# Which attention heads of a hybrid decoder layer get turned exponentials

## The chip, the cores and the metric

One core of one Trainium2 chip runs the whole layer. The metric is the device time of one execution in microseconds (us); lower is better. The profiled execution has a span (first to last instruction) and a time of its own, which is a little longer.

## The reference, cut to what matters

One decoder layer on `x` of 2048 tokens by 1024 channels. After an RMS norm one input projection feeds three head groups, each with a SiLU gate; their gated outputs are mapped back by an output projection and added to `x`.

```python
# eight causal heads of 64 channels, with a forget gate
logits = (q . k) / sqrt(64) + F[t] - F[s]        # F = cumsum(log sigmoid(f)), only s <= t
y_b = softmax(logits) @ v
# four memory heads: every query reads 256 memory tokens
y_m = softmax((q_m . k_m) / sqrt(64)) @ v_m
# a pooling mixer, four groups
y = x + concat(y_a * silu(g_a), y_b * silu(g_b), y_m * silu(g_m)) @ w_out
```

All of it is float32; the kernel keeps that precision by splitting operands into a high and a low fp16 half.

## The kernel before, in words

The work is cut into 16 units n = (p, j): four passes p, each with two causal heads (h = 0 and h = 1) and one memory head (h = 2), and in each pass four query blocks j of 512 queries. `proj` computes one unit's projections on TensorE (`mm3`, L721: tiles `pa` of 512 columns and `pb` of 256). `attention` then takes the three heads of a unit in the order 2, 0, 1. After the last unit comes the output projection (`po`, also L721), whose early part is placed beside the last attention units.

A causal head in block j has 16j + 10 score blocks of 128 queries by 128 keys that lie on or below the diagonal: 10, 26, 42 and 58. A memory head has 8. A head is softened in one of two ways.

**The normal way** (`scores`, `soften`). Queries lie on the partitions, keys in the free dimension. TensorE writes a PSUM tile `q` of up to 1024 score columns with two matmuls per piece of up to 512 columns (L1250 and L1256: the high half and the correction), and the diagonal blocks get a mask matmul (L1253). VectorE takes the minimum of each row (L1273), `nm` is made from it (L1281, L1277), and ScalarE takes the exponential with `nm` as its bias (L1288). `halves` splits the result into a high half (L1308 on VectorE or L1311 on ScalarE) and a low half (L1315 on VectorE or GpSimd), both in a tile `ph`. The weighting with the values needs keys on the partitions, so a DMA transposes `ph` to `pt` (L1324), issued from SyncE's queue, and only then do the `pv` matmuls of `weigh` (L1353 to L1355, three for each block) run. Heads of j >= 2 are softened in two groups of keys (the first 1024, and the rest), which are joined at the end with a factor `al` (L1296, L1298, L1371, L1386).

**The turned way** (`scores` with `peak=True`, `peak`, `turned_scores`, `spread`). The scores are written twice. First with queries on the partitions and the high half alone (L1250 and the mask, no L1256), only to take the row minima (L1180, L1184); when all pieces of the head have been read, the minima of two groups are merged (L1194), scaled into two rows `mz` (L1196, L1197), transposed by four matmuls into `mp` (L1204) and copied into two spare rows of the query tile (L1208). Then the scores are written again with keys on the partitions (`columns`, L1166 and L1170, the mask at L1168), so that the minimum is subtracted by the matmul itself and the exponential (L1223) needs no bias of its own per query. The split halves in `ph` are already in the form that `weigh` wants: no transpose by DMA, no `pt`, and one group of keys.

`turned(j, h)` chooses the way. It is read where the heads are listed (L1431), and by `follow` (L1516), which sets how fast attention is paced against the projections.

The order of all work is planned at build time by `Order`, a simulation with a cost for each engine and for SyncE's queue (`COST`, L40); instructions are then issued in the planned order, and each engine runs its own list in order. TensorE's list merges `lead` (projections) and `follow` (attention) with a lag of 1.1 units. `AHEAD = 1` lets the minima pass of the next head be issued while the current head is still in its exponentials:

```python
            for ahead in todo[:self.AHEAD + 1]:
                ...
                if ahead["todo"]:
                    step = ahead
                    break
```

Score tiles `q` have two buffers, `ph` nine, `pt` six, and up to `DEEP = 7` parts wait in the queue `late` before their `pv` matmuls are drained, first in, first out. SyncE's queue also issues the loads of `x`, of the weights, the stores and the transposes of `Q`, `K` and the mixed rows. When the three heads of a unit are finished, `store_mixed` casts and stores the unit's mixed rows (L1531, two casts per unit).

Of the kernel before, what the change touches and what calls it, by code (L numbers as in the profile page):

```python
# [201 lines left out]
class Layer:  # L202
# [932 lines left out]

    def turned(self, j, h):

        return h == 2 or j < 2

    def columns(self, j, h):  # L1140

# [269 lines left out]
    def attention(self):  # L1411
# [15 lines left out]
        def heads():  # L1427
            for n in range(n_units):
                p, j = divmod(n, NJ)
                for h in (2, 0, 1):  # L1430
                    turned = self.turned(j, h)  # L1431
                    peaks = self.pieces(j, h)
                    pieces = self.columns(j, h) if turned else peaks
                    subs, count = [], 0
                    for piece in pieces:
                        subs.append([])
                        for sub in piece if turned else self.cut(piece):
                            subs[-1].append((count, sub))
                            count += 1
                    yield {  # L1440
                        "n": n, "h": h, "turned": turned, "todo": list(enumerate(peaks)) if turned else [], "peaks": len(peaks),
                        "rest": list(enumerate(pieces)), "pv": {}, "box": {}, "subs": subs, "count": count, "last": h == 1,
                        "flat": [sub for group in subs for _, sub in group],
                    }
# [310 lines left out]
```

## Time and profile before

| what | value |
|---|---|
| time, median of 3 runs | 1100.43 us (1099.67 to 1102.37) |
| the profiled execution: time | 1099.49 us |
| the profiled execution: span | 1097.6 us |
| TensorE busy | 1019.0 us, 93% |
| VectorE busy | 821.7 us, 75% |
| ScalarE busy | 563.6 us, 51% |
| GpSimd busy | 454.7 us, 41% |
| the DMA queue of SyncE | 76.2% of the 16 engines' span |
| mean granted TensorE clock | 0.990 |

Busy shares are means over stages with different limits, and the end of a matmul in the trace is modelled, so a stretch in which TensorE is busy need not be one at its full rate. The work of one pass alternates between light attention (blocks 0 and 1) and heavy attention (blocks 2 and 3), so the views are read by such stretches.

### The profile page before, as it was taken

The numbers are of one execution on the slowest core, as the hardware profiler recorded it, in microseconds if no ns is written. First come the engines' busy times: TensorE is split into PE (matmuls) and PEld (weight loads), VectorE is DVE, ScalarE is ACT, GpSimd is POOL, SyncE is SP. The second block draws the span as 40 slices with busy tenths as digits, with TensorE's granted clock in tenths as the row PEclk, the third lists the DMA queues.
The fourth block names the chain that finished last, engine by engine and source line by source line (L and its number), as shares of the span: only waits on it lengthen the run. The fifth ranks groups of instructions, "written<-read, shape, count | busy, mean of one in ns | idle before, by whom it ended". The sixth has DMA issues, their size and how long they took to land.

```text
span 1097.6 us, 23751 instructions
## 1 busy us (share of the span) xinstructions
PE 1019.0 (93%) x8981; PEld 615.1 (56%) x8981; DVE 821.7 (75%) x1894; ACT 563.6 (51%) x1424; POOL 454.7 (41%) x504
## 2 busy tenths in 40 slices
PE   6799998899889998898999999989999979999998
PEld 2355655556556565565565655556656645554443
DVE  6976879996987986969987969799796895761111
ACT  4775757665555455647544656655555663430000
POOL 6654636444544544535443434444533351221000
PEclk9999999999999999999999999999999999999999
DMA  9988677895996627969968159899692696998521
GB/s 280 222 213 190 181 220 189 211 185 124 199 205 172 172 79 131 180 144 180 198 182 217 40 113 182 192 212 199 196 222 62 143 209 168 226 219 215 182 96 48
DMA packets 375361, 192.05 MB, mean 175 GB/s; under 512 B 331792, under 2 KB 339920, under 8 KB 374224
## 3 DMA queue, kind: packets, MB, share of 16 engines
q1 hardware_dynamic: 375104, 190.54, 76.2%
q8 instruction: 70, 1.15, 0.4%
q14 instruction: 43, 0.35, 0.1%
q10 hardware_dynamic: 144, 0.01, 0.0%
HBM read 84.23 MB, written 25.26 MB: 100 GB/s over the span
## 4 chain that ended last, share of the span: by engine, by line
PE 34%; DVE 20%; DMA 11%; issue 4%; POOL 2%; ACT 2%; SPq 1%; DVEq 0%; ACTq 0%; POOLq 0%
PE po L721 13%; DMA pt<-ph 9%; PE pa L721 7%; PE pb L721 6%; DVE mn L1273 4%; DVE ph L1315 4%; DVE ph L1308 2%; PE q L1250 2%; PE pv L1353 2%; PE pv L1355 1%; DMA w1a<-in_w_a 1%; PE pv L1354 1%; DVE mn L1184 1%; PE q L1256 1%; DVE qq L1013 1%
## 5 line engine op out<-in xcount | busy, mean ns | idle before, releaser
L721 PEld LDWEIGHTS <-x 128*128 128x128 f16 x2304 | 216.3, 98 | 131.2 <-issue 3.8
L721 PE MATMUL pa<-ah,x 128*128 128x512 f16 x768 | 250.0, 381 | 0.4 <-DVE z L960 0.4
L1315 POOL TENSOR_TENSOR ph<-p,ph 128x512 f16<-128x512 f32 (+3 forms) x114 | 134.7, 1185 | 240.0 <-DVE ph L1308 117.6
L1288 ACT ACTIVATE p<-q,nm 128x512 f32<-128x512 f32 (+1 forms) x224 | 135.4, 644 | 124.7 <-DVE nm L1277 52.5
L721 PE MATMUL po<-aho,om 128*128 128x512 f16 x512 | 159.2, 381 | 2.9 <-DVE xo L1619 2.9
L1315 DVE TENSOR_TENSOR ph<-p,ph 128x512 f16<-128x512 f32 (+2 forms) x214 | 149.1, 716 | 2.4 <-ACT ph L1311 1.4
L721 PE MATMUL pa<-al,x 128*128 128x512 f16 x384 | 146.2, 381 | 0.0
L1273 DVE TENSOR_REDUCE mn<-q 128x1 f32<-128x1024 f32 (+7 forms) x128 | 124.6, 983 | 27.9 <-PE q L1256 27.7
L721 PE MATMUL pb<-bh,x 128*128 128x256 f16 x768 | 142.0, 273 | 1.3 <-DVE v L940 1.3
L1353 PE MATMUL pv<-v,pt 128*128 128x65 f16 x800 | 94.6, 194 | 33.2 <-DMA pt<-ph 32.5
L721 PEld LDWEIGHTS <-om 128*128 128x128 f16 x768 | 73.5, 98 | 87.1 <-issue 4.1
L1353 PEld LDWEIGHTS <-pt 128*128 128x128 f16 x800 | 74.9, 98 | 60.3 <-DMA pt<-ph 49.4
L1250 PE MATMUL q<-k,q 67*128 67x512 f16 (+2 forms) x320 | 104.6, 350 | 3.4 <-DVE mn L1184 1.4
L721 PE MATMUL pb<-bl,x 128*128 128x256 f16 x384 | 104.9, 273 | 0.0
L985 POOL TENSOR_TENSOR rr<-ss,mhalf 128x10 f32<-128x10 f32 x32 | 63.7, 1990 | 98.2 <-DVE ss L980 83.2
L721 PE MATMUL po<-alo,om 128*128 128x512 f16 x256 | 97.5, 381 | 0.0
L1405 POOL TENSOR_TENSOR gate<-gate,hy 128x128 f32<-128x128 f32 x96 | 51.7, 558 | 106.4 <-DVE hy L1396 96.3
L1354 PE MATMUL pv<-v,pt 128*128 128x64 f16 x800 | 94.1, 194 | 0.0
L1355 PE MATMUL pv<-v,pt 128*128 128x65 f16 x800 | 93.8, 194 | 0.0
L1619 DVE SCALAR_TENSOR_TENSOR xo<-po,So_p,xo 128x512 f32<-128x512 f32 x32 | 23.9, 748 | 92.1 <-PE po L721 92.1
L721 PEld LDWEIGHTS <-xx 128*128 128x128 f16 x720 | 68.0, 98 | 42.9 <-PE pa L745 1.2
L1311 ACT CAST ph<-p 128x512 f16<-128x512 f32 (+2 forms) x162 | 90.6, 584 | 1.6
(275 smaller groups left out, 2292.8 us busy)
## 6 DMA issues: line engine op xcount, KB each, us to landing
x<-xd SPq DMA_DIRECT2D x48, 512.0 KB, 5.7
xrx<-in_x SPq DMA_DIRECT2D x16, 512.0 KB
xd<-xx SPq DMA_DIRECT2D x16, 512.0 KB, 6.3
md<-mt SPq DMA_DIRECT2D x32, 256.0 KB, 2.3
om<-md SPq DMA_DIRECT2D x8, 1024.0 KB
xo<-in_x SPq DMA_DIRECT2D x16, 512.0 KB, 6.2
out_dram<-xo SPq DMA_DIRECT2D x32, 256.0 KB, 3.4
w0a<-in_w_a SPq DMA_DIRECT2D x12, 512.0 KB, 4.9
```

Of the source, the lines that this page charges most:

```text
L721: nc.tensor.matmul(out, rows, r[kt][:, :ncol], start=(kt == 0 and i == 0), stop=(kt == KT - 1 and i == 2))
L985: nc.gpsimd.tensor_tensor(rr, ss, self.mhalf[:, 0:10].rearrange("p (a b) -> p a b", b=5), op=ALU.pow)
L1250: nc.tensor.matmul(out, q1, kb, start=bank not in used, stop=peak and not diag, **kw)
L1273: nc.vector.tensor_reduce(mn[:, g, i:i + 1], qk[:, off:off + w], axis=AX.X, op=ALU.min)
L1288: nc.scalar.activation(p32[:, at:at + w], qk[:, off:off + w], AF.Exp, bias=nm[:, g, i:i + 1], scale=-1.0)
L1311: nc.scalar.copy(hl[:, :w], p32[:, :w])
L1315: (nc.vector if eng == "V" else nc.gpsimd).tensor_tensor(hl[:, w:2 * w], p32[:, :w], hl[:, :w], op=ALU.subtract)
L1353: nc.tensor.matmul(pv[:, i, :], ph, hi, start=start and b == 0, stop=False, **kw)
L1354: nc.tensor.matmul(pv[:, i, 0:HD], ph, v[:, 0:HD], start=False, stop=False, **kw)
L1355: nc.tensor.matmul(pv[:, i, :], pl, hi, start=False, stop=end and b == nb - 1, **kw)
L1405: nc.gpsimd.tensor_tensor(gate, gate, y[:, 2 * u:2 * u + 2, 0:HD], op=ALU.mult)
L1619: nc.vector.scalar_tensor_tensor(xr[:, t, :], pj, self.So, xr[:, t, :], op0=ALU.mult, op1=ALU.add)
```

## The change

One line. The memory heads stay turned. Before, both causal heads of blocks 0 and 1 were turned and both of blocks 2 and 3 normal. After it, the first causal head (h = 0) of blocks 1, 2 and 3 is turned, and the second head of every block and both heads of block 0 are normal.

```diff
     def turned(self, j, h):
 
-        return h == 2 or j < 2
+        return h == 2 or (h == 0 and j > 0)
```

## Rows read from the trace of the kernel before

**Rows 1.** The page: the span and the busy time of each engine.
```profile
span 1097.6 us, 23751 instructions
PE 1019.0 (93%) x8981; PEld 615.1 (56%) x8981; DVE 821.7 (75%) x1894; ACT 563.6 (51%) x1424; POOL 454.7 (41%) x504
```

**Rows 2.** Tile `mh`: the casts that end a unit; duration min/median/max, first and last start.
```profile
L1531 ACT CAST mh<-gate x32: 602/626/651, 129.2 to 996.1; 128x512 f16<-128x512 f32 x32
```

**Rows 3.** Windows: stretch, length, busy of each engine, clock, DMA share, GB/s.
```profile
129.20:191.50 62.30, 56.79 (x512) 35.98 (x511) 53.89 (x131) 40.88 (x97) 35.80 (x43) 1.00 0.75 199
191.50:347.30 155.80, 143.66 (x1432) 92.03 (x1431) 134.04 (x325) 89.46 (x234) 73.58 (x75) 0.99 0.91 184
347.30:408.50 61.20, 59.58 (x579) 37.95 (x576) 53.01 (x123) 34.07 (x91) 30.91 (x37) 1.00 0.50 137
408.50:562.20 153.70, 141.53 (x1384) 89.75 (x1383) 123.86 (x291) 84.88 (x229) 69.31 (x74) 0.98 0.85 164
562.20:630.40 68.20, 66.56 (x643) 42.90 (x641) 57.32 (x136) 37.66 (x101) 29.70 (x33) 1.00 0.53 142
630.40:781.80 151.40, 140.43 (x1424) 89.97 (x1422) 127.64 (x291) 87.60 (x234) 64.34 (x71) 1.00 0.89 178
781.80:843.90 62.10, 60.55 (x580) 38.67 (x579) 51.46 (x119) 35.24 (x95) 29.77 (x35) 1.00 0.60 164
843.90:995.60 151.70, 142.37 (x1289) 80.67 (x1288) 106.86 (x217) 69.56 (x152) 46.80 (x52) 0.99 0.88 192
995.60:1097.60 102.00, 98.05 (x455) 44.26 (x452) 14.69 (x20) 1.14 (x2) 2.64 (x3) 0.99 0.40 126
```

**Rows 4.** The chain that ended last: start, us, what.
```profile
993.93 99.73 PE po L721 x462
```

**Rows 5.** TensorE's waits by line: us in total, times, longest us.
```profile
PE pv L1353 <- DMA pt<-ph: 32.5, 39, 2.7
PE pv L1355 <- DVE ph L1315: 2.9, 8, 0.7
```

**Rows 6.** Tile `pt`: issues on SyncE's queue (ns min/median/max), and their landing.
```profile
L1324 SPq DMA_TRANSPOSE pt<-ph x216: 1167/1272/4282, 207.5 to 989.6; - x108
DMA to landing us min/median/max: 2.5/3.5/6.8
```

**Rows 7.** Groups by form on TensorE: busy us, mean ns of one.
```profile
L1253 PE MATMUL q<-mask,identb 128*128 128x128 bf16 x128 | 28.4, 224 | 0.0
L1204 PE MATMUL mp<-identh,mz 128*128 128x128 f16 x128 | 12.5, 220 | 4.1 <-DVE mz L1197 3.0 <-DVE hy L1371 0.8 <-DVE gate L1579 0.3
```

**Rows 8.** Groups by form on VectorE and ScalarE.
```profile
L1273 DVE TENSOR_REDUCE mn<-q 128x1 f32<-128x1024 f32 x72 | 87.7, 1218 | 22.9 <-PE q L1256 22.8
L1196 DVE TENSOR_SCALAR mz<-mn 128x4 f16<-128x4 f32 x32 | 7.2, 225 | 0.1
L1197 DVE SCALAR_TENSOR_TENSOR mz<-mz,mn 128x4 f16<-128x4 f16 x32 | 8.9, 278 | 1.1
L1208 ACT CAST q<-mp 2x512 f16<-2x512 f32 x25 | 14.4, 577 | 38.8 <-PE mp L1204 38.3
L1281 DVE TENSOR_SCALAR nm<-mn 128x1 f32<-128x1 f32 x64 | 9.8, 154 | 2.2
L1277 DVE SCALAR_TENSOR_TENSOR nm<-mn,nm 128x1 f32<-128x1 f32 x40 | 11.8, 295 | 1.4
L1371 DVE TENSOR_TENSOR hy<-pv,al 128x260 f32<-128x260 f32 x16 | 6.8, 423 | 9.4 <-PE pv L1355 9.4
L1386 DVE TENSOR_TENSOR hy<-hy,pv 128x260 f32<-128x260 f32 x16 | 6.7, 421 | 14.4 <-PE pv L1355 14.4
L1288 ACT ACTIVATE p<-q,nm 128x512 f32<-128x512 f32 x176 | 116.2, 690 | 113.2 <-DVE nm L1281 43.9 <-DVE nm L1277 43.8 <-PE pv L1355 8.0
L1288 ACT ACTIVATE p<-q,nm 128x128 f32<-128x128 f32 x16 | 6.0, 372 | 10.3 <-DVE nm L1277 8.7 <-POOL ph L1315 1.4 <-DVE ph L1315 0.2
L1223 ACT ACTIVATE p<-q,lnp 128x512 f32<-128x512 f32 x96 | 61.7, 686 | 42.2 <-PE q L1170 32.0 <-issue 3.6 <-POOL ph L1315 2.9
```

## The prediction

> **What bounds the kernel now.** I read the page first, then cut the span into stretches, then asked for the waits and the chain. The page puts TensorE at 93%, far above VectorE's 75% [rows 1], but such a share is a mean, so the stretches matter. I end a stretch where a unit's mixed rows are cast, two casts per unit from 129.2 us on [rows 2]; 347.3, 408.5 and so on are such ends. That gives long stretches in which the attention of query blocks 2 and 3 ends, and short ones for blocks 0 and 1 [rows 3]. The projections run through both.
>
> In the four long stretches (612.6 us together) TensorE is busy 568.0 us and idle 44.6, or 7.3%; the DMA share is 0.85 to 0.91. In the three short ones from 347.3 on (191.5 us) it is idle 4.8, or 2.5%, at a DMA share of 0.50 to 0.60 [rows 3]. What differs is seen in the waits: TensorE's only large one is the first weighting matmul waiting for a transpose, 32.5 us in 39 waits; the next wait in that attention, for VectorE's low halves, is 2.9 us [rows 5]. All transposes belong to normal heads, and all of these stood in blocks 2 and 3. The end is TensorE alone: the chain's last long piece is 462 output matmuls in 99.73 us [rows 4], one every 0.216 us. So the time is TensorE's stream plus the holes in it, and the change touches both: it puts matmuls into the stream and takes transposes out of the holes.
>
> **The change, counted in score blocks.** Per pass, the causal blocks that are turned go from 2 x 10 + 2 x 26 = 72 to 26 + 42 + 58 = 126; those that pass through a transpose go from 2 x 42 + 2 x 58 = 200 to 2 x 10 + 26 + 42 + 58 = 146. Turned causal heads go from four to three. In place, blocks 2 and 3 lose 100 of 200 transposed blocks, and blocks 0 and 1 gain 46 where there were none.
>
> **TensorE's stream: +9.9 us.** A turned block costs one more matmul of 128 columns (the minima pass; the scores themselves and the weighting have as many columns either way). At 0.216 us for 512 columns [rows 4] that is 0.054 us: 54 x 0.054 = 2.92 us per pass. One turned head fewer saves four `mp` matmuls and four mask matmuls of 128 columns: the 0.22 us of one such row [rows 7] is latency, the columns cost 0.054 each, so 8 x 0.054 = 0.43. Net 2.48 per pass, 9.9 in four: blocks 2 and 3 get 100 x 0.054 plus 16 matmuls more, blocks 0 and 1 lose the rest. The price is at most this; at least it is nothing, if it falls into holes.
>
> **VectorE: about -14 us of work, ScalarE about none.** The minima read as many columns either way (1.22 us for 1024). In block 2 a turned head drops four `nm` of 0.154, two of 0.295, and the joining of two groups, 0.423 + 0.421: 2.05 us. It adds `mz`, 0.225 + 0.278, and one merge of minima, which has no row; between nothing and the 0.42 of the joining, I take the nearest in size, 0.225. That is -1.32; block 3 with four `nm` of 0.295 gives -1.91. In block 0 two heads drop `mz` and take two `nm`, -0.39; block 1, +0.11. Per pass -3.5 [rows 8]. On ScalarE a turned head's exponentials come in full pieces (0.686 against 0.690 for 512 columns), so only the number of small ones moves: +2 in block 0, +1 in block 1, -1 in each of 2 and 3. Each costs about 0.27 beyond its columns (0.372 for 128 columns less a third of 0.690 - 0.372), against one 0.577 copy fewer [rows 8]. I cost ScalarE at nothing.
>
> **The DMAs: 23 us of full DMA time less per pass.** Issues go from 54 per pass (216 [rows 6]) to 3 + 3 + 8 + 11 + 16 = 41, so SyncE's queue is 4 x 13 x 1.27 = 66 us less occupied, and what stands behind a transpose in it (loads of `x`, the next transposes) goes out earlier. For the transfers: the short stretches hold no such transpose and move 137 GB/s at a share of 0.50, or 142 at 0.53, or 164 at 0.60: about 272 GB/s when full. The stretch from 408.5 us has 153.7 x 0.85 = 130.6 us of full DMA time and moves 25.2 MB [rows 3]. The 200 transposed blocks with both halves are 13.1 MB; the other 12.1 MB at 272 GB/s take 44.5 us, which leaves 86 us, or 0.43 us per block. Blocks 2 and 3 then lose 100 x 0.43 = 43 us, and their DMA share falls to (130.6 - 43)/153.7 = 0.57; a short stretch gains 46 x 0.43 = 20 us and rises from 0.50 to 0.82.
>
> The Trainium skill ("Advanced Engine Details and Errata", X-Bar Transpose (TRN2)) says that transposing DMAs run as fast as regular ones. By that rule 100 blocks would give back only 6.55 MB / 272 GB/s = 24 us, the long stretches would stand at 0.69 and the short ones at 0.64, all of them well below full, and the sum would lack the +12 below and come to 1077. The trace disagrees: share rises far more than bytes once the transposes run.
>
> **The holes: -20 us.** In the long stretches the excess over the short ones is 44.6 - 0.025 x 612.6 = 29.3 us. With the DMA share at 0.57, where the short ones stand today, I let all of it go: -29.3. If the holes only follow the number of transposes, half goes: -14.6. In the short stretches (253.8 us with the one from 129.2) the share rises to that of the long ones, so I give them the long ones' excess rate, 4.8%: +12.0; if holes follow the number of transposes, 184 x 29.3/800 = +6.7. That makes -17.3 (or -7.9). A hole is also longer than the trace draws it: a matmul's row is drawn to its modelled end, about 0.16 us past its last column, so each wait that vanishes gives some 0.16 more. With 52 of 216 transposes fewer plus the shorter landing, about half of the 39 waits [rows 5] go: -3. VectorE's 14 us are not added: it is 80 to 86% busy in three of the long stretches [rows 3] and ahead of TensorE's list.
>
> Sum: 1099.49 + 9.9 - 17.3 - 3 = 1089.1; the profiled execution lies 0.9 below the median, within its spread. I say 1089.
>
> **The rivals.** *TensorE has room (0.20).* The added matmuls of the minima pass wait for no transpose, so they can be what TensorE does in the holes that remain. Then the +9.9 costs nothing: 1079. The dense tail at one matmul every 0.216 us speaks against a slack rate; the 37.6 us of holes that my sum leaves from 129.2 us on (44.6 + 4.8 + 5.5 - 17.3) speak for it. The Trainium skill ("Perfetto Trace Analysis", Identifying the Most-Contended Engine) judges TensorE by its weight loads, not by matmul busy time, and these are busy 56% [rows 1]: by that rule there is room. The tail has them busy 44.26 of 102 us [rows 3] at full rate, so here a low share of weight loads is no sign of room.
>
> *Nothing to measure (0.14).* The holes only follow the number of transposes: 9.9 - 7.9 = +2.0 us, 1101.5. For it: a list in order stalls at each late transpose, however empty the queues. Against: a landing of 3.5 us in the median and 6.8 at most, against 2.5 at best [rows 6], shows queueing.
>
> *Slower (0.26).* A turned head may not start its exponentials before all its minima are read: six tiles of 1.22 us in block 2 and eight in block 3 [rows 8], 7.3 and 9.8 us in which VectorE reduces and ScalarE has only the small memory head. A normal head reduces one tile while the exponentials of the last one run. Behind the last of them wait `mz`, `mp` and the copy, and behind these every exponential and every `pv` part of the head. Four such pairs are 68 us. Covered by projections and by the previous unit's parts in `late`, they cost nothing; uncovered for 15% they eat the gain of 10.4; for 25% the time is 1089 + 17 = 1106. For it: VectorE at 134.0 of 155.8 us in the first long stretch [rows 3]. Against: block 1 does this today with four tiles per head, twice in a unit, and its stretches have the fewest holes.
>
> **How the numbers follow.** My forecast (1083 to 1096) has a chance of 0.40, the room on TensorE 0.20 (1073 to 1083), no difference 0.14 (1097 to 1103), slower 0.26 (1104 to 1110; the upper end is all of the +9.9 with no hole closed). What a measurement of this kernel tells from no change is about 0.3%, 3.3 us. So faster 0.60, same 0.14, slower 0.26. Two tenths are left out at 1074 below and 1106 above; the forecast's own range is 1083 to 1096.
>
> **What will show it.** In the profile after: 164 transposes of `pt`, landing in about 3 us; TensorE's wait for `pt` well under 20 us; DMA share near 0.6 in the stretches of blocks 2 and 3 and near 0.8 in those of 0 and 1; TensorE's idle share in the long stretches near 3%. It is wrong in price if the matmul stream grows by other than 10 us, and wrong in kind if the wait for `pt` goes but idle time at score tiles (waits of L1166 or L1250 for minima, copies or exponentials) takes its place.

## The result, and the profile after

The changed kernel takes 1110.75 us in the median of 4 runs (1109.46 to 1113.56), against 1100.3 for the kernel before on the same chip: a ratio of 1.0086, interval 1.0057 to 1.0116. It is slower by about 0.9%, where I forecast 1.0% faster, and lies outside my range.

The page of the changed kernel, its span and the busy time of each engine, and its DMA queue of SyncE (packets, MB, share of the 16 engines' span):

```profile
span 1107.7 us, 23556 instructions
...
PE 1028.8 (93%) x8997; PEld 618.3 (56%) x8997; DVE 841.3 (76%) x1913; ACT 545.1 (49%) x1379; POOL 422.7 (38%) x474
...
q1 hardware_dynamic: 318144, 176.37, 68.5%
```

TensorE is busy 9.8 us longer than before [rows 1]; I had worked out 9.9. That the two agree is partly luck: the mean granted clock is also lower, 0.986 after 0.990, and the clock's part is set apart below. The DMA share fell from the 76.2% of the table above to 68.5%. Taken of each kernel's own span that is 836 and 759 us of full DMA time, 78 us less; I had worked out 93. What did not come is the closing of the holes: span less busy time is 78.9 us, against 78.6 before.

TensorE's waits in the changed kernel (us in total, times, longest us), and its issues of transposes (duration in ns min/median/max, first and last start):

```profile
PE pv L1353 <- DMA pt<-ph: 29.3, 35, 2.0
PE mp L1204 <- DVE mz L1197: 8.1, 8, 4.2
...
PE pv L1355 <- DVE ph L1315: 3.1, 5, 1.3
```

```profile
L1324 SPq DMA_TRANSPOSE pt<-ph x164: 1190/1261/3960, 111.2 to 986.0; - x164
```

There are 164 transposes as counted, but the wait for them went only from 32.5 to 29.3 us [rows 5]: 39 waits at 216 transposes, 35 at 164. I had also forecast a landing in about 3 us. The view gives no landing for the changed kernel, and for the kernel before it matched only 28 of the 216 issues of [rows 6]. An estimate from the traces, which takes the last step of each transfer's semaphore before that semaphore's next use as the landing, gives a mean from issue to landing of 3.9 us over all 216 transposes before, and of 4.1 us over the 164 now. The landing did not get shorter.

The windows of the changed kernel, ended where a unit's mixed rows are cast, as in [rows 3] (stretch, length, busy of PE, PEld, DVE, ACT and POOL, clock, DMA share, GB/s):

```profile
0.00:214.70 214.70, 183.38 (x1286) 108.07 (x1287) 170.87 (x421) 131.47 (x321) 118.95 (x141) 0.95 0.90 223
```

```profile
214.70:352.00 137.30, 130.14 (x1374) 85.83 (x1373) 118.48 (x282) 81.67 (x206) 62.47 (x65) 0.99 0.66 136
352.00:417.40 65.40, 61.78 (x560) 38.26 (x558) 52.94 (x128) 34.16 (x97) 30.84 (x35) 1.00 0.79 177
417.40:570.50 153.10, 145.23 (x1469) 93.74 (x1468) 132.59 (x304) 84.32 (x222) 58.87 (x64) 0.99 0.58 125
570.50:636.50 66.00, 62.61 (x561) 38.21 (x560) 53.40 (x128) 33.46 (x96) 31.19 (x36) 1.00 0.80 181
636.50:791.70 155.20, 145.42 (x1444) 92.02 (x1442) 135.02 (x306) 83.65 (x221) 57.12 (x64) 0.99 0.64 145
791.70:856.80 65.10, 60.02 (x559) 37.09 (x560) 47.92 (x111) 31.98 (x92) 28.87 (x33) 1.00 0.82 173
856.80:993.00 136.20, 129.25 (x1246) 74.94 (x1244) 113.55 (x216) 63.22 (x131) 31.74 (x38) 1.00 0.65 147
```

The DMA shares are what I expected, 0.58 to 0.66 in the four long stretches and 0.79 to 0.82 in the three short ones. The holes are not. In the long stretches (581.8 us) TensorE is idle 31.8, or 5.5%: 12.8 less than before, not 29.3. Of its wait for `pt`, 19.1 us stand there, where all of the 32.5 stood before: 0.048 us for each transposed block, after 0.041. The estimated landing in these stretches is 4.1 us in the mean, after 3.9, although the DMA share fell from 0.85 to 0.91 down to 0.58 to 0.66. In the short ones (196.5 us) it is idle 12.1, 7.3 more. Up to the end of block 1 in the first pass it is idle 31.3 of 214.7 us, where before it was 25.2 of the first 191.5 (the page's 78.6 less the 53.4 of all later windows in [rows 3]). The sums cancel, and the 9.8 us of busy time remain.

### The profile page after: what moved, and what is told of

Its sections match the earlier page's. It is cut to its first block, busy times and chain, and to the rows that moved or that the text cites. A ratio compares the mean times of both kernels' runs of the same rounds, so it can differ in the third digit from the quotient of the medians.

```text
span 1107.7 us, 23556 instructions
## 1 busy us (share of the span) xinstructions
PE 1028.8 (93%) x8997; PEld 618.3 (56%) x8997; DVE 841.3 (76%) x1913; ACT 545.1 (49%) x1379; POOL 422.7 (38%) x474
## 3 DMA queue, kind: packets, MB, share of 16 engines
q1 hardware_dynamic: 318144, 176.37, 68.5%
## 5 line engine op out<-in xcount | busy, mean ns | idle before, releaser
L721 PE MATMUL pa<-ah,x 128*128 128x512 f16 x768 | 253.9, 381 | 0.6 <-ACT mh L1531 0.4
L1315 POOL TENSOR_TENSOR ph<-p,ph 128x512 f16<-128x512 f32 (+3 forms) x92 | 105.9, 1157 | 209.0 <-DVE ph L1308 122.0
L1315 DVE TENSOR_TENSOR ph<-p,ph 128x512 f16<-128x512 f32 (+2 forms) x236 | 167.3, 732 | 2.0
L1288 ACT ACTIVATE p<-q,nm 128x512 f32<-128x512 f32 (+3 forms) x176 | 101.5, 621 | 89.0 <-DVE nm L1281 46.0
L1223 ACT ACTIVATE p<-q,lnp 128x512 f32<-128x512 f32 (+1 forms) x164 | 104.4, 673 | 60.8 <-PE q L1170 44.1
L1308 DVE CAST ph<-p 128x512 f16<-128x512 f32 (+3 forms) x205 | 97.9, 490 | 8.1 <-ACT p L1223 3.9
L1250 PE MATMUL q<-k,q 67*128 67x512 f16 (+2 forms) x320 | 98.9, 347 | 3.6 <-DVE mn L1180 1.2
L1353 PE MATMUL pv<-v,pt 128*128 128x65 f16 x584 | 69.5, 194 | 29.9 <-DMA pt<-ph 29.3
L1273 DVE TENSOR_REDUCE mn<-q 128x1 f32<-128x1024 f32 (+4 forms) x112 | 92.5, 844 | 4.6 <-PE q L1256 4.3
L1353 PEld LDWEIGHTS <-pt 128*128 128x128 f16 x584 | 54.8, 99 | 53.0 <-DMA pt<-ph 45.8
L1184 DVE TENSOR_REDUCE mn<-q 128x1 f32<-128x1024 f32 (+4 forms) x80 | 77.0, 988 | 2.3 <-PE q L1253 1.7
```

Source lines behind the costliest of these rows:

```text
L721: nc.tensor.matmul(out, rows, r[kt][:, :ncol], start=(kt == 0 and i == 0), stop=(kt == KT - 1 and i == 2))
L1184: nc.vector.tensor_reduce(mn[:, g, i:i + 1], qk[:, off:off + w], axis=AX.X, op=ALU.min)
L1223: nc.scalar.activation(p32[:, :w], qk[:, b * TB:b * TB + w], AF.Exp, bias=self.lnp, scale=-1.0)
L1250: nc.tensor.matmul(out, q1, kb, start=bank not in used, stop=peak and not diag, **kw)
L1273: nc.vector.tensor_reduce(mn[:, g, i:i + 1], qk[:, off:off + w], axis=AX.X, op=ALU.min)
L1288: nc.scalar.activation(p32[:, at:at + w], qk[:, off:off + w], AF.Exp, bias=nm[:, g, i:i + 1], scale=-1.0)
```

## The experiments

Theory 1 after the result: TensorE's stream counts in full, and the holes follow the number of transposed blocks, whatever the DMA share. Theory 2, my forecast's: the holes come from busy DMA queues. Theory 3, the rival that had slower in it: turned heads of blocks 2 and 3 pay for waiting for all their minima. Later theories come where they arose. Each ratio below is to the kernel before on the same chip. "Idle" is span less TensorE's busy time.

### The two halves, none, and a doubled minima pass

Half A alone, `part_a`:

```diff
-        return h == 2 or j < 2
+        return h == 2 or (h == 0 and j == 1)
```

> One half of the change alone: blocks 0 and 1 give up three of their four turned heads per pass, blocks 2 and 3 stay normal. Minima matmuls fall by 46 score blocks and three heads' small matmuls per pass: 4 x (46 x 0.054 + 3 x 0.43) = 15.1 us less TensorE stream; 184 more blocks pass through a transpose in all. Theory 1 (TensorE's stream counts in full, and its holes follow the number of transposed blocks, 0.037 us each, however busy the DMAs are): -15.1 + 6.7 = -8.4, about 1092. Theory 2 (holes come from busy DMA queues): short stretches reach the holes of the long ones, 4.8% of 250 us, and the DMA share over the span rises to 0.83: -15.1 + 12 or more, 1097 or above. Theory 3 (turned heads in blocks 2 and 3 pay for waiting for all their minima): no such head here, so about 1092 too.

Half B alone, `part_b`:

```diff
-        return h == 2 or j < 2
+        return h == 2 or j < 2 or h == 0
```

> The other half alone: the first causal head of blocks 2 and 3 is turned as well, blocks 0 and 1 stay all turned. Minima matmuls grow by 100 score blocks and two heads' small matmuls per pass: 4 x (5.4 + 0.86) = 25 us more TensorE stream; 400 blocks less through a transpose. Theory 1: 25 - 14.6 = +10.4, about 1111. Theory 2 (busy queues): all 29 us of the long stretches' extra holes go, nothing is added elsewhere: 25 - 29 = -4, about 1096. Theory 3: the stream's 25 us and waits for minima on top, with no hole closed: 1118 or above, and TensorE's wait for the minima rows (L1204, L1166) several times that of the kernel before.

No causal head turned, `none_turned`:

```diff
-        return h == 2 or j < 2
+        return h == 2
```

> No causal head is turned, only the memory heads. TensorE's stream falls by 4 x (72 x 0.054 + 4 x 0.43) = 22.4 us against the kernel before; 288 more blocks pass through a transpose, and the DMA share over the span rises from 0.76 to about 0.87. Theory 1: -22.4 + 10.5 = -12, about 1088. Theory 2: every stretch has the holes of the long ones or more, 18 us or more added, and the time is 1096 or above, with TensorE's wait for transposes at 60 us or more. Theory 3: like theory 1, since no minima pass of a causal head is left to wait for.

The changed kernel with the minima pass doubled, `double_minima`:

```diff
+                if peak and h < 2:
+                    nc.tensor.matmul(out, q1, kb, start=True, stop=True, **kw)
-                nc.tensor.matmul(out, q1, kb, start=bank not in used, stop=peak and not diag, **kw)
+                nc.tensor.matmul(out, q1, kb, start=bank not in used or (peak and h < 2), stop=peak and not diag, **kw)
```

> The changed kernel with each matmul of the causal heads' minima pass issued twice into the same place, the second over the first; the planner is not told, so the order on every engine stays that of the changed kernel. 126 score blocks per pass, 4 x 126 x 0.054 = 27 us of TensorE stream more. If TensorE's stream counts in full (theory 1): +27 against the changed kernel, about 1137. If the minima pass runs in holes that TensorE has anyway: less than +10, below 1121.

| kernel | transposed blocks per pass | median us, ratio (interval) | TensorE busy | of that lost to the low clock (estimate, see below) | idle | wait for `pt` |
|---|---|---|---|---|---|---|
| before | 200 | 1100.3 | 1019.0 | 9.5 | 78.6 | 32.5 |
| changed | 146 | 1110.75, 1.0086 (1.0057 to 1.0116) | 1028.8 | 13.5 | 78.9 | 29.3 |
| half A | 246 | 1113.63, 1.0107 (1.0062 to 1.0152) | 1012.9 | 19.4 | 95.9 | 43.7 |
| half B | 100 | 1104.85, 1.0038 (1.0015 to 1.0062) | 1041.6 | 11.9 | 61.8 | 10.9 |
| none turned | 272 | 1108.34, 1.0076 (1.0053 to 1.0099) | 1004.3 | 16.1 | 98.3 | 44.1 |
| minima doubled | 146 | 1130.34, 1.0265 (1.0230 to 1.0299) | 1058.1 | 15.3 | 74.1 | 29.7 |

Half A takes matmuls away and gets slower; half B adds the most and, in these orders, is better than the change that holds both. Theory 3 falls with half B: its time is far below the 1118 that it needed. These are TensorE's waits there for transposes, for low halves, and for the minima rows, which are the least of the three:

```profile
PE pv L1353 <- DMA pt<-ph: 10.9, 17, 2.9
...
PE pv L1355 <- DVE ph L1315: 7.9, 16, 1.1
...
PE mp L1204 <- DVE mz L1197: 2.1, 5, 0.8
```

Theory 1 holds for the wait in these five: 10.9, 29.3, 32.5, 43.7, 44.1 us at 100, 146, 200, 246, 272 blocks rises with the blocks at every step. It fails for the time of half A (1092 expected) and of none turned (1088); both lie where theory 2 put them, at 1096 to 1097 or above, and far above. Theory 2 misses too: it wanted a wait for transposes of 60 us or more with none turned, which has 44.1. The doubled minima cost 1.0265 less 1.0086, 1.79% or 19.7 us, of the 27 that their columns take; between the two profiled executions it is 24.5 us, busy time 29.3 more and idle 4.8 less. So an added minima matmul costs 0.7 to 0.9 of its columns, not nothing.

Busy time is more than columns. By the count half A should have lost 15.1 us of it and lost 6.1, and none turned 22.4 and lost 14.7. Their mean granted clock is 0.979 and 0.981, against 0.990 before, and wherever a record of these traces is below 1.00 it is at 0.50, the 1.2 GHz level. The estimate in the table adds up, over windows of 2 us, TensorE's busy time times what the granted clock lacks to 1. Without that part the busy time moves against the kernel before by -15.9 us for half A (counted -15.1), -21.3 for none turned (counted -22.4), +20.3 for half B (counted +25) and +5.9 for the changed kernel (counted +9.9), and with the minima doubled by +27.4 against the changed kernel (counted 27). So the count of columns holds roughly even where the time went the other way. What makes half A and none turned slow is 17.3 and 19.7 us more of idle time and about 10 and 7 us more at the low clock.

### The first pass, and the landing that the plan assumes

Two suspects were left. The changed kernel lost at the start (theory A: in the crowded first pass normal heads in blocks 0 and 1 are dear). And a wait that stays while the queues empty could be the plan's own: the matmuls of `pv` may stand in TensorE's list before their transpose can have landed (theory C). `turned` was given the pass p for the first two of these; the planned landing has a constant.

The first pass as before, later ones changed, `first_pass_old`:

```diff
-        return h == 2 or j < 2
+        return h == 2 or (j < 2 if p == 0 else h == 0 and j > 0)
```

> The first pass keeps the old choice (both causal heads of blocks 0 and 1 turned), passes 2 to 4 have the changed one. In the traces the changed kernel ended its first pass at 352.0 us against 347.3 (last unit's cast), and held 17 us of holes up to the end of block 1 of that pass against 9. If that loss belongs to the first pass's crowded start (theory A): the first pass ends near 347, the rest takes the 755.7 us of the changed kernel, about 1105. If the changed kernel loses evenly over its passes through TensorE's stream (theory B, 2.5 us a pass): 1110.75 - 2.5, about 1108; if the start costs whatever the choice, the same 1108 to 1110.

The first pass as before, later ones with no causal head turned, `later_passes_none`:

```diff
-        return h == 2 or j < 2
+        return h == 2 or (p == 0 and j < 2)
```

> The first pass keeps the old choice; in passes 2 to 4 only the memory heads are turned. From the end of the first pass on, the kernel with no causal head turned took 746.0 us, the kernel before 750.3, the changed one 755.7. Theory A (a normal head in blocks 0 and 1 is dear in the first pass only): 347.3 + 746.0 and 1.9 around the span, about 1095, faster than both kernels. Theory B (holes follow the DMA share, which rises to about 0.87 in passes 2 to 4): no faster than the kernel before, 1100 or above.

The changed kernel and the one before with a later landing, `later_landing_new` and `later_landing_old`:

```diff
-MARGIN = 0
+MARGIN = 1.0
```

> The changed kernel, with the planner told that each transpose of the attention lands 1.0 us later (MARGIN 1.0 for 0). Theory C (TensorE's holes at transposes come from a plan that puts the weighting matmuls too early, not from full DMA queues): TensorE's wait for transposes falls from 29 us below 12, and the time by 8 us or more, to 1102 or below. If the holes are set by what TensorE has to do at all (other work is short, or VectorE decides), the wait moves elsewhere and the time stays within 0.3% of 1110.75.

> The kernel before, with the same later landing in the plan. Theory C: TensorE's wait for transposes falls from 32.5 us below 14, and the time by 8 us or more, to 1092 or below. Otherwise it stays within 0.3% of the kernel before, with the wait elsewhere.

First pass as before: 1100.85, ratio 1.0006 (0.9986 to 1.0026), where theory A gave 1105. Later passes with none: 1097.97, 0.9976 (0.9956 to 0.9997), between the 1095 of theory A and the 1100 of the other, with the wait for `pt` at 44.9 us (254 blocks per pass in the mean). Later landing in the changed kernel: 1093.32, 0.9951 (0.9928 to 0.9973). Later landing in the kernel before: 1107.09, 1.0074 (1.0050 to 1.0099). TensorE's wait for transposes in the last two, the changed kernel first:

```profile
PE pv L1353 <- DMA pt<-ph: 11.6, 16, 1.8
```

```profile
PE pv L1353 <- DMA pt<-ph: 33.1, 28, 4.1
```

In the changed kernel the wait goes from 29.3 to 11.6 with the DMA share where it was (68.3%): there it depends on where the plan puts the matmuls that use the transpose. By the kernel's constants the plan gives a transpose of 512 columns 2.98 us from issue to landing on a free queue, where the estimates above are 3.9 and 4.1 us. In the kernel before the wait stays, in fewer and longer pieces, up to 4.1 us; why is not shown, as the landing estimated for that run, 4.0 us, is no other. Its span is 9.2 us longer, of which 7.2 are busy time of the same 8981 matmuls at a mean granted clock of 0.980 for 0.990. Theory C is right for the one and wrong for the other.

### Do the remedies add up, and is block 0 the place?

`first_old_later_landing` is `first_pass_old` with `MARGIN = 1.0`, `b_later_landing` is half B with it, `landing_two` is the changed kernel with `MARGIN = 2.0`. `first_block_old`:

```diff
-        return h == 2 or (h == 0 and j > 0)
+        return h == 2 or (h == 0 and j > 0) or (p == 0 and j == 0)
```

> The first pass with the old choice, later passes with the changed one, and the plan's transposes landing 1.0 us later: the two remedies together. Theory A and C independent: 1110.75 - 9.9 - 17.4, about 1083. If the later landing already mends the start (its first pass ended at 344.5 us, against 352.0 in the changed kernel and 347.3 in the one before): no better than the later landing alone, 1090 to 1094. If the later landing harms normal heads that share full DMA queues, as in the kernel before: worse than 1094.

> The other half alone (blocks 0 and 1 all turned, the first causal head of 2 and 3 too), with the later landing. Its wait for transposes was only 10.9 us without. Theory C: what can be won is at most that wait and what hangs on it, 5 to 10 us, about 1097. Rival: the order is drawn anew and moves the time by several us either way whatever the wait.

> The changed kernel with landings planned 2.0 us later. Theory C: TensorE's wait for transposes, 29.3 us at 0 and 11.6 at 1.0, falls further, below 8, and the time stays at or below 1094. Rival (the gain at 1.0 was a lucky order, not the wait): the wait or the time does not follow, and the time is back at 1100 or above.

> The changed kernel, but in the first pass both causal heads of block 0 are turned as well, as before. If the start's loss comes from block 0's normal heads (their transposes stand among the first loads, and unit 1 begins late): about 1102, the unit of block 1 in the first pass ending near 194 us as in the kernel before (214.7 in the changed one). If it comes from block 1 (one head turned, one normal): about 1110.

The two remedies together: 1101.21, 1.0002 (0.9986 to 1.0017), where independent remedies would give 1083. The wait for `pt` fell from 30.0 to 18.1 us and the time not at all. Half B with the later landing: 1103.17, 1.0021 (1.0011 to 1.0032), its wait 11.0 as before, where theory C gave about 1097. Landing 2.0 us later in the changed kernel: 1092.71, 0.9918 (0.9900 to 0.9936), the fastest of all. Its waits:

```profile
PE mp L1204 <- DVE mz L1197: 8.6, 8, 2.8
...
PE q L1250 <- DVE mn L1180: 7.0, 5, 2.3
...
PE pv L1353 <- DMA pt<-ph: 3.8, 5, 1.7
```

The wait for transposes is all but gone; against the landing 1.0 us later, 7.8 us of it went and the waits for minima grew, so the time hardly moved: 0.6 us between the medians, 0.3% between the ratios. Only block 0 as before in the first pass: 1113.55, 1.0112 (1.0094 to 1.0131). By this order block 0 is not the place; what one order can say comes next.

### What an order alone is worth

That the remedies did not add up called for a control: the same kernels with the planner nudged too little to matter, so that it draws another order of the same work. `nudge_new` and `nudge_old` have `MARGIN = 0.1`, `nudge2_new` and `nudge2_old` have 0.2. `first_01_old` differs from `first_block_old` by one head:

```diff
-        return h == 2 or (h == 0 and j > 0) or (p == 0 and j == 0)
+        return h == 2 or (h == 0 and j > 0) or (p == 0 and j < 2)
```

and `first_01_old_later` is that with `MARGIN = 1.0`.

> The changed kernel, but in the first pass all causal heads of blocks 0 and 1 are turned as before (its blocks 2 and 3 keep the changed choice). It differs from the run with only block 0 as before by one head: the second head of block 1 in the first pass. If that mixed block is what the start loses on: about 1101 to 1104, the holes up to the end of block 1 near 33 us instead of 41. If the loss lies in blocks 2 and 3 of the first pass: 1110 or above.

> The same with landings planned 1.0 us later. If the remedies add up where half of the heavy heads are turned throughout: 1085 to 1090, the fastest of all. If the later landing had already mended the start: 1090 to 1094. If they cancel as in the run with the whole first pass as before: about 1101.

> The changed kernel with landings planned 0.1 us later: the order is drawn anew, the wait should hardly change. If the gain at 1.0 us was the wait: TensorE's wait for transposes 24 to 32 us and the time within 4 us of 1110.75. If any new order moves the time by as much: 10 us or more either way.

> The kernel before with the same nudge of 0.1 us. The spread of its time about 1100 is the worth of an order alone: within 4 us if orders are alike, 8 us or more if the kernel before is itself a lucky draw.

> The kernel before with landings planned 0.2 us later: its third order. If the order drawn decides (theory D: the choice of heads is worth less than 4 us either way, and the kernel before was a lucky draw): 1103 to 1112. If 0.1 was the odd one: within 4 us of 1100.5.

> The changed kernel with the same nudge of 0.2 us. Theory D: anywhere from 1095 to 1108, no longer slower than the kernel before with the same nudge. If the change itself costs its 9.9 us of TensorE stream in every order: 8 us or more above the kernel before with the same nudge.

| order | before: median, ratio (interval); busy; idle; wait for `pt` | changed: the same |
|---|---|---|
| 0 | 1100.3, 1; 1019.0; 78.6; 32.5 | 1110.75, 1.0086 (1.0057 to 1.0116); 1028.8; 78.9; 29.3 |
| 0.1 | 1111.74, 1.0107 (1.0067 to 1.0147); 1022.4; 90.3; 39.0 | 1103.9, 1.0034 (1.0013 to 1.0055); 1026.7; 73.3; 25.0 |
| 0.2 | 1103.89, 1.0013 (0.9994 to 1.0031); 1022.2; 80.0; 33.9 | 1105.08, 1.0028 (1.0007 to 1.0048); 1026.6; 76.8; 23.4 |
| mean | ratio 1.0040; 1021.2; 83.0; 35.1 | ratio 1.0049; 1027.4; 76.3; 25.9 |

The pages of the nudged kernel before (0.1), where the kernel has the same instructions on TensorE as [rows 1] and a span 15.1 us longer, and of the nudged changed one:

```profile
span 1112.7 us, 23769 instructions
...
PE 1022.4 (92%) x8981; PEld 615.8 (55%) x8981; DVE 828.4 (74%) x1894; ACT 557.0 (50%) x1408; POOL 469.5 (42%) x520
```

```profile
span 1100.0 us, 23539 instructions
...
PE 1026.7 (93%) x8997; PEld 618.7 (56%) x8997; DVE 847.6 (77%) x1921; ACT 545.2 (50%) x1376; POOL 418.4 (38%) x469
```

A nudge of 0.1 us in one planned latency, which leaves the work alone but for a few operations dealt to another engine, costs the kernel before 1.07% and gives the changed one back 0.5%. Over three orders each the choices differ by 0.0009, about 1 us, with orders that scatter by 7 to 11. So the 10.4 us between the two kernels are no more than the order alone moves either of them, and can't be called the change's. Nor do three orders each show that the change is worth nothing: by their scatter the difference of 1 us is uncertain by about 4 us (its standard error). Theory D of the expectations, that the order decides, held for both kernels at 0.2; at 0.1 the changed kernel has the wait that theory C gave it, 25.0 us, and not the time. What the choice does shows in the means: TensorE busy 6.2 us more, idle 6.7 us less, and a wait for transposes of 25.9 against 35.1 us, a ratio of 0.74, where the transposed blocks stand at 146/200 = 0.73.

Cut into the stretches of [rows 3], TensorE's idle time (us, orders 0, 0.1 and 0.2) keeps the two kernels apart in every order:

| stretches | before | changed | difference of the means |
|---|---|---|---|
| up to the end of block 1 in the first pass | 25.2, 27.6, 25.5 | 31.3, 32.6, 32.3 | +6.0 |
| the four long ones | 44.6, 50.9, 42.1 | 31.8, 28.4, 31.1 | -15.4 |
| the three short ones | 4.8, 7.9, 8.1 | 12.1, 8.6, 9.6 | +3.2 |

The busy time without the part at the low clock, by the same estimate, is 1009.5, 1010.0 and 1006.8 us before and 1015.4, 1016.0 and 1017.3 in the changed kernel: 7.5 us more.

Blocks 0 and 1 of the first pass as before: 1098.73, 0.9985 (0.9961 to 1.0010); with the later landing 1098.08, 0.9973 (0.9954 to 0.9992), the wait down from 22.2 to 13.2 us and the time unmoved. The first lies below the 1101 to 1104 that a dear block 1 would give. Windows up to the end of block 1 in the first pass, for `first_01_old`, the nudged kernel before, and the nudged changed one (0.1):

```profile
0.00:192.20 192.20, 168.09 (x1214) 100.94 (x1215) 154.47 (x381) 123.85 (x295) 107.82 (x131) 0.96 0.81 213
```

```profile
0.00:193.60 193.60, 166.02 (x1214) 99.31 (x1215) 155.26 (x381) 123.76 (x295) 107.24 (x131) 0.98 0.81 211
```

```profile
0.00:216.80 216.80, 184.22 (x1283) 109.05 (x1284) 173.68 (x420) 131.09 (x320) 117.18 (x141) 0.95 0.89 221
```

With the old choice in blocks 0 and 1 of the first pass TensorE is idle 24.1 and 27.6 us up to there (25.2 before); with the changed one 32.6 (31.3 in the order of the result). This part of the loss, 4 to 8 us, stands in these orders, though the stretch is 21 to 25 us longer and so holds some idle time of later work. Whether it is the reason why `first_01_old` and `first_pass_old` are some 10 us faster than the changed kernel can't be told: the orders scatter by as much. With the later landing the changed kernel idles 25.4 us up to there (26.5 at 2.0), with no head changed back. The 17 and 9 us, or 41 and 33, that the expectations name for these holes are not what the windows give.

## Why the prediction was wrong

**TensorE's stream, +9.9:** near in size, and the 9.8 us that the busy time rose in the result's order are luck in part: by the estimate 5.9 of them are columns and the rest is the low clock. Over three orders busy time rose by 6.2 us, its columns by 7.5. The price per column held with the minima doubled (27.4 us of 27 in busy time); in the time they cost 0.7 to 0.9 of it. The clock had no term in the sum.

**VectorE, -14:** wrong in sign. Its busy time rose from 821.7 to 841.3 us. I counted the fixed operations and left out that the plan deals the halves of `ph` out to the engine that it thinks is free. These are the low halves of 512 columns, on VectorE and on GpSimd, first in the kernel before and then in the changed one (busy us, mean ns of one | idle before):

```profile
L1315 DVE TENSOR_TENSOR ph<-p,ph 128x512 f16<-128x512 f32 x178 | 132.3, 761 | 2.3 <-ACT ph L1311 1.4
...
L1315 POOL TENSOR_TENSOR ph<-p,ph 128x512 f16<-128x512 f32 x94 | 115.9, 1237 | 198.0 <-DVE ph L1308 101.0 <-ACT ph L1311 72.8 <-issue 13.0
```

```profile
L1315 DVE TENSOR_TENSOR ph<-p,ph 128x512 f16<-128x512 f32 x207 | 152.5, 757 | 2.0
...
L1315 POOL TENSOR_TENSOR ph<-p,ph 128x512 f16<-128x512 f32 x61 | 78.7, 1297 | 134.4 <-DVE ph L1308 83.0 <-ACT ph L1311 38.9 <-issue 3.6
```

GpSimd was busy 454.7 us before [rows 1] and is 422.7 now. The sum did not use the -14, so nothing else fell with it.

**The DMAs, 23 us per pass:** right in the main: 78 us of 93 in all, or 0.36 us per block for 0.43, and the shares of both kinds of stretch as worked out. In the paragraph on transposes at the plain rate the short stretches would stand at 0.68, not 0.64 (46 blocks are 3.0 MB, 11 us of 61.2); nothing hangs on it.

**The holes, -20: the step that failed.** The term "With the DMA share at 0.57, where the short ones stand today, I let all of it go: -29.3" measured -12.8. Over three orders it is -15.4, with no order of the one kernel among those of the other. That is my lower bound of -14.6, holes that follow the number of transposes, which I had set aside. The term for the rest, +12.0, came out as +11.9 in the stretches that it meant (7.3 in the short ones, 4.6 in the one from 129.2 us), with another 1.5 before them. The -3 for the undrawn ends of holes counted on a shorter landing and on half of the 39 waits going; four went. So the holes gave nothing where I had -20, and 1089 became about 1109, which the profiled execution took.

What I had wrong is that a busy DMA share makes the landing late. I read queueing out of a landing of 3.5 us in the median and 6.8 at most; by the estimate the landing takes as long in the long stretches at a share of 0.58 to 0.66 as at 0.85 to 0.91, and so each transposed block that is left costs about what it did. What moves the wait in the changed kernel is the plan: at an unchanged DMA share it is 29.3, 25.0, 23.4, 11.6 and 3.8 us as the planned landing is 0, 0.1, 0.2, 1.0 and 2.0 us later. An order that asks for the data too early waits just as long on an emptier queue. That the landing does not depend on the share rests on the estimate; that the holes did not go with the share is measured in three orders.

**The rivals.** *Nothing to measure* gave 1101.5 by the mechanism that the traces bear out: the wait, and the idle time of the long stretches, follow the transposed blocks. Over three orders the choice moves the time by about 1 us, give or take 4. *TensorE has room* is at most a third true by the doubled minima. *Slower* came about in the order of the result, but not by its mechanism: the waits for the minima rows (L1204) grew from 3.0 [rows 7] to 8.1 us in the changed kernel, 4.24 of them in one place of the first pass, while half B, with as many turned heads in blocks 2 and 3, waited only 2.1 us for them. Half A, with none there, waited 7.8 us with a longest wait of the same 4.2.

**What was not in the sum at all:** the order. I took the holes of one drawn order for a property of the choice of heads. Three orders of the same kernel spread over 11.4 us before and 6.9 us after, about as much as the effect that I forecast; my range allowed for no such term.

**What stays open.** Why the later landing gave 8 us or more by the ratios in the changed kernel (two runs, both below all its three orders) and no more than 2 us in the four other kernels that had it, two of which lost 9 to 12 us of wait by it; these may be draws as well. Why half B waits only 0.027 us for each transposed block, where the changed kernel waits 0.036 to 0.048 over its three orders, in long stretches of the same choice. And whether half A and none turned, one order each, are slow by choice or by draw; that they wait and idle more than the kernel before follows the blocks.

## What to carry to other kernels

Where a planner writes each engine's order, a kernel's time is one draw: before an edit of under 2% is believed, nudge a planned latency by too little to matter and see how far the time moves, in both kernels. A wait for a transfer is relieved by less traffic only if the traffic made it late; look whether the landing and the waits shrink with the share, or only the number of waits, and try moving the consumer later in the order first. Here that cut the wait in three kernels of five and the time clearly in one. Matmul work that is added to a list near full costs most of its columns. Before a busy time is read as work, look at the granted clock: the same matmuls took 7.2 us longer in another order whose mean clock was 0.980 for 0.990.

## What the runs showed of the hardware

The 4.24 us wait in the first pass of the changed kernel is a chain of small things. Its timeline on VectorE, then on GpSimd, then on TensorE (start us, us, what):

```profile
156.99 1.22 DVE L1184 TENSOR_REDUCE mn<-q 128x1 f32<-128x1024 f32 x1
158.13 1.21 DVE L518 TENSOR_REDUCE wacca<-w0a 128x2 f32<-128x1024 f32 x1
...
159.71 0.71 DVE L1196 TENSOR_SCALAR mz<-mn 128x4 f16<-128x4 f32 x1
160.46 1.07 DVE L1197 SCALAR_TENSOR_TENSOR mz<-mz,mn 128x4 f16<-128x4 f16 x1
```

```profile
159.24 2.26 POOL L1315 TENSOR_TENSOR ph<-p,ph 128x512 f16<-128x512 f32 x2 [7.86 <-ACT ph L1311]
```

```profile
161.59 0.61 PE L1204 MATMUL mp<-identh,mz 128*128 128x128 f16 x4 [4.24 <-DVE mz L1197]
```

Two operations on 4 columns take 0.71 and 1.07 us, where L1196 and L1197 have minima of 157 and 175 ns in the same trace. They end at 160.42 and 161.53 us, and GpSimd's two subtractions, which run from 159.24 to 161.50, are about 1.13 us each, so they end at about 160.4 and at 161.5: each small operation ends as one of GpSimd's does. The Trainium skill ("SBUF — State Buffer", SBUF: two separate sides) says that VectorE and GpSimd share a pair of ports that GpSimd, or a VectorE instruction with two inputs in SBUF or in a two-port mode, holds for a whole instruction while the other waits. The trace agrees with it here for L1197, which reads two tiles in SBUF; whether L1196 runs in a two-port mode no run shows.

The two operations took 1.44 us more than their minima, a third of the wait. The rest is VectorE reading the last minima until 158.21 us, and other work, of the weights and the gates, that stands ahead of the two in its list until 159.71. The same wait of 4.24 us comes back near 163 us in half A and in both nudged changed kernels, so it goes with the turned head of block 1 in the first pass and not with one order.

After that wait TensorE ran slow. The window behind it in the changed kernel (clock in the last column but two):

```profile
161.59:167.00 5.41, 5.40 (x38) 3.27 (x38) 4.70 (x13) 3.26 (x5) 2.94 (x2) 0.50 0.63 125
```

TensorE is busy throughout at a granted clock of 0.50, the 1.2 GHz level. Before it fell, the engine had stood idle for 4.24 us. The matmuls of 512 columns follow each other 0.43 us apart there (from 163.24 us on), and 0.22 us apart before the wait (from 156.32 us on). So a wait of 4.24 us was followed by half the rate for more than 5 us.
